# A two-layer hybrid attention block: dividing by the softmax sums after the product with the values

## The chip, the cores and the metric

The kernel runs on one core of one Trainium2 chip. The metric is the device time of one execution in microseconds (us). Three runs of the kernel before gave 601.19, 601.36 and 601.63 us, median 601.36. A core has a matrix engine (PE in the rows; PEld is its loading of the stationary operand), VectorE (DVE), ScalarE (ACT), GpSimd (POOL), SyncE (SP) that issues nearly all DMAs here, and 16 DMA engines. Every engine works through its own queue in order and waits for others by semaphores.

## The reference

Two layers of width 1024 over 256 tokens, in fp32. Each layer norms x, projects it to 2824 columns, runs three mixers side by side, projects their outputs back, and adds an MLP (1024 to 4096 to 1024, squared relu). The mixers are block attention ("moba", 6 heads of 64; with 256 tokens and blocks of 256 it is plain causal attention), a chunked linear recurrence ("mlstm", 4 heads), and sliding-window attention ("swa", 6 query heads on 2 key heads, window 128, with a sink per head). The change is in the two softmax mixers:

```
p = softmax(concat([s_sel, s_own]))          # moba: causal rows of 256 keys
o = einsum('bhql,bhld->bhqd', p, v)
...
p = softmax(concat([s, sink]))[..., :-1]     # swa: the sink is in the sum alone
o = einsum('bnkgqj,bnjkd->bnqkgd', p, vb)
```

Queries and keys are rms-normed per head and rotated before. Since the sum of a row of numerators is one number per query and head, dividing the numerators by it or dividing the product by it gives the same result.

## The kernel before, in words

**Weights.** All weight matrices come from HBM in units of up to 512 KB by one queue (SP). Each unit is split into a high part (ScalarE, a rounded copy, line 258) and a low part (VectorE, a subtraction, line 265), and each product is three matmuls: high by high, high by low, low by high (`three`, lines 613 to 615). The same split is made of the activations. There are eight buffers for high parts and seven for low ones.

**The order.** The program is written as many generators (one for each projection part, head, pair of heads, block of the MLP). A `Scheduler` (lines 127 to 230) with a model of each engine's costs and latencies (`LATENCY`, `ISSUE`, `SWITCH`) picks at each step the operation that can start first by its model, and among those that can start within a short time of it the one with the lowest rank. The result is one fixed instruction order for each engine; on the chip only semaphores hold. Generators of layer 1 have ranks 1000 above those of layer 0. The splits of weight units have rank -20 if the unit is the next one to be used, and 90 otherwise, in either layer (`split_rank`, line 393); the first five units have about -50.

**A pair of heads** (`pair`, line 1093, and `head`, line 1142): twelve pairs in all, three of moba and three of swa in each layer. TensorE makes the scores of both heads, each head in 64 rows of the array. For each head, VectorE scales, masks and takes the row maximum with one custom operation for each of the two query blocks (128 and 256 keys); the scale is a negated inverse root, `nrq`, made by a multiplication by -1 of `rq`. ScalarE takes the exponentials and their sums `su`; in swa the exponential of the sink is added. VectorE takes the reciprocals, and the numerators are multiplied by them in place: two operations for a head, of 128 and 256 columns, on VectorE or on ScalarE, whichever the model has free. TensorE turns the three 128x128 tiles (`to_T`, line 679), ScalarE copies them back to SBUF. The product with the values (`values`, line 1125) then takes 64 columns of the values as the stationary operand and streams the turned numerators past it, 256 and 128 columns, the two heads side by side in the two halves of the array's columns. The result is already turned, [2 heads x 64, 256 queries], and is split at once into the operand of the output projection.

**Around the pairs.** While pairs wait for VectorE and ScalarE, TensorE works on the later projection parts and on the first chunks of the output projection (`mix`, line 1187). When `mix` is done, x is updated (VectorE), turned (`turn`, line 568, TensorE, rank -29) and the MLP starts (`up_first`).

**Roots** (`inverse_root`, line 518): exp(-0.5 ln v) on ScalarE, then one Newton step in three small VectorE operations. `roots` (line 1028) makes those of the queries and keys and then `nrq`.

Of the kernel before, what the change touches and what calls it, by code (L numbers as in the profile page):

```python
# [13 lines left out]
AF = mybir.ActivationFunctionType  # L14
OP = mybir.AluOpType
# [5 lines left out]
HD = 64  # L21
# [102 lines left out]
            self.cur = None  # L124


LATENCY = {"PE": 0.20, "ACT": 0.145, "DVE": 0.13, "POOL": 0.15, "DMA": 1.0}
ISSUE = {"PE": 0.235, "ACT": 0.0, "DVE": 0.0, "POOL": 0.0, "DMA": 0.0}
SWITCH = 0.2
SOON = {"PE": 0.08, "ACT": 0.2, "DVE": 0.05, "POOL": 0.0, "DMA": 0.0}  # L130


class Scheduler:
# [27 lines left out]
    def run(self):  # L161
        while self.threads:
# [38 lines left out]
            if best is None:  # L201
                if not self.threads:
# [4 lines left out]
            t0, eng = best[0], best[1].engine  # L207
            t, th, op = min((c for c in ready if c[2].engine == eng and c[0] <= t0 + SOON[eng]),
                            key=lambda c: c[1].rank())
            self.now = max(self.now, t0)  # L210
            op.fn()
            end = t + op.cost * (1 + (eng == "PE" and t < self.cold))
# [22 lines left out]
def tile_hybrid_block(ctx: ExitStack, tc: tile.TileContext, x, xT, smalls, w_in, w_out, w_up,  # L235
# [36 lines left out]
    def stt(waits, o, a, s, b, op0, op1):  # L272
        return dve(waits, free_size(o),
                   lambda: V.scalar_tensor_tensor(o, a, s, b, op0=op0, op1=op1), pointers=(s,),  # L274
                   bank=bank_of(a, b))
# [6 lines left out]
        return (yield tt([t] + waits, lo, src, f32(hi), OP.subtract).ranked(rank))  # L282

    def dma(waits, nbytes, o, i, eng=None):
        return Op("DMA", nbytes / 360e3, waits, lambda: (eng or nc.sync).dma_start(o, i))

    PS = buffers("ps", 8, [128, 512], F32, pp)
    TMP = buffers("tmp", 6, [128, 512])
# [84 lines left out]
    def load_units():  # L373
        for k, u in enumerate(units):
# [15 lines left out]
            u.t = yield dma([t], u.n * 512, dst, u.src)  # L390
            u.there.signal(u.t)

    def split_rank(k):
        u = units[k]
        if k < 5:
            return -50 + u.kc0
        return lambda: -20 if k < in_use[0] + URGENT else 90

    def split_units():
        for k, u in enumerate(units):  # L400
# [97 lines left out]

    def small_loads(l, after):

        yield Wait(*after)
        g = tab[l][:, T_GB:T_SINK].rearrange("p (s i d) -> p s i d", s=2, i=4)
        t = max(e.t for e in after)
        for k, o in enumerate((cg, sg)):
            for i in range(4):
                t = yield dve([t], 128, lambda k=k, o=o, i=i: V.scalar_tensor_tensor(
                    o[:, i], rope_t[:, k], 1.0 if i % 2 else HD ** -0.5,
                    g[:, k, i, None, :].to_broadcast([128, 2, HD]), op0=OP.mult, op1=OP.mult))
        t = yield ts([t], nsink, tab[l][:, T_SINK:T_BIAS], -1.0, None, OP.mult)
        small_ev[l].signal(t)  # L510
# [7 lines left out]
    def inverse_root(waits, v, k, eps, dst):  # L518


        e, ke = eps or (0.0, 0.0)
        iy, y, t0 = yield from small()
        it, r, t1 = yield from small()
        n = free_size(v)
        y, r = y[:, :n], r[:, :n]
        t = yield act([t0, *waits], y, v, AF.Ln, scale=1.0 / k, bias=e)
        t = yield act([t], y, y, AF.Exp, scale=-0.5)
        t = yield stt([t, t1], r, y, -0.5 / k, y, OP.mult, OP.mult)
        t = yield stt([t], r, v, ke, r, OP.add, OP.mult)
        t = yield stt([t], dst, r, 1.5, y, OP.add, OP.mult)  # L530
        SMALL.put(iy, t)
        SMALL.put(it, t)
        return t
# [168 lines left out]
    for b in range(2):  # L702
        G.memset(vaug[b][:, :, 64:65], 1.0)
    rq = {k: const(f"rq_{k}", [128, 2, 12]) for k in "ms"}
    nrq = {k: const(f"nrq_{k}", [128, 2, 6]) for k in "ms"}
    ssq = {k: const(f"ssq_{k}", [128, 2, 12]) for k in "ms"}
    gcol = const("gcol", [128, 2, 4])
    ecol = const("ecol", [128, 2, 4])
# [3 lines left out]
    class Layer:  # L712
        def __init__(self, l, x_in):
            self.l, self.p, self.x_in = l, plan[l], x_in
            self.h1 = [[Event() for _ in range(KC)] for _ in range(2)]
            self.h2 = [[Event() for _ in range(KC)] for _ in range(2)]
            self.y = [Event(2 if c in (3, 4) else 1) for c in range(8)]
            self.yb = [None] * 4
            self.yuses = [0] * 4
            self.x_mid, self.x_out = ([[Event() for _ in range(4)] for _ in range(2)]  # L720
                                      for _ in range(2))

            groups = (0, 1, 2, "s")
            self.qT = {k: Event(2) for k in ("sq", "sk", 0, 1, 2)}
            self.vv = {k: Event(2) for k in ("mv", "sv", "va", "sig")}
            self.lq = [Event(), Event()]
            self.gates_in = Event(2)
            self.rows, self.cols, self.ecol = Event(), Event(), Event()
            self.row = Event()
            self.ssq = {k: [Event(2 if k == "s" else 1) for _ in range(2)] for k in groups}  # L730
            self.rq = {k: [Event(), Event()] for k in groups}
            self.nrq = {k: [Event(), Event()] for k in groups}
# [295 lines left out]
        def roots(self, g, tb):  # L1028

            yield Wait(self.ssq[g][tb], self.st[tb])  # L1030
            st = stat[1][tb]
            k, a, n, nq = ("s", 0, 8, 6) if g == "s" else ("m", 4 * g, 4, 2)
            r = rq[k][:, tb, a:a + n]
            t = yield from inverse_root([self.ssq[g][tb], self.st[tb]], ssq[k][:, tb, a:a + n],
                                        float(HD), (st[:, 1:2], st[:, 3:4]), r)
            self.rq[g][tb].signal(t)
            t = yield ts([t], nrq[k][:, tb, a // 2:a // 2 + nq], r[:, 0:nq], -1.0, None, OP.mult)
            self.nrq[g][tb].signal(t)

        def moba_part(self, i, tb):  # L1040

# [51 lines left out]
        def pair(self, swa, i, gate, prio):  # L1093

            heads = (i, i + 3) if swa else (2 * i, 2 * i + 1)
            qT, kT = (sqT, skT) if swa else (mT[:, 0], mT[:, 1])
            evs = [self.qT[k] for k in (("sq", "sk") if swa else (i,))]
# [16 lines left out]

            t = yield pe([tp for _, tp in banks] + evs, 0.66, scores, "rows")
            pT = {}
            for h, (ip, _) in zip(heads, banks):
                sch.add(prio + h, self.head(swa, h, pT, done, ip, t))  # L1120
            yield Wait(done, vev)
            iy, ty = yield Get(PS)
            yps = PS.tiles[iy]

            def values():
                for o, blk, cols in ((slice(0, 256), 0, slice(0, 256)),
                                     (slice(128, 256), 1, slice(256, 384))):
                    for n, h in enumerate(heads):
                        d = (n if swa else h) * HD
                        T.matmul(yps[64 * n:64 * n + 64, o], vv[blk][:, d:d + HD],  # L1130
                                 MID.tiles[pT[h]][:, cols], start=blk == 0, stop=blk == 1)

            t = yield pe([done, ty, vev], 0.68, values, "columns").ranked(prio)
            for h in heads:
                MID.put(pT[h], t)
            gate.put(ig, t)
            hi, lo, ty = yield from self.y_tile(c)
            t = yield from split([t, ty], hi, lo, yps[:, 0:256])
            PS.put(iy, t)
            self.y[c].signal(t)  # L1140

        def head(self, swa, h, pT, done, ip, t):
# [5 lines left out]
            nm, su, es = sm[:, 0:2], sm[:, 2:4], sm[:, 4:6]  # L1148
            cuts = (slice(0, 128), slice(128, 384))
            g, hq = ("s", h % 3 * 2 + h // 3) if swa else ("m", h)  # L1150
            done_q = self.nrq["s" if swa else h // 2]
            mask, least = (mask_s, nsink[:, h:h + 1]) if swa else (mask_m, -NEG)
            yield Wait(*done_q)

# [1 line left out]
            for k, cut in enumerate(cuts):  # L1156
                w = [t, t0, tm, *done_q] + ([small_ev[self.l]] if swa else [])
                t = yield dve(w, cut.stop - cut.start + 60, lambda k=k, cut=cut: V.tensor_tensor_reduce(  # L1158
                    p[:, cut], ps[:, cut], mask[:, cut], nrq[g][:, k, hq:hq + 1], least,
                    OP.add, OP.min, nm[:, k:k + 1]), pointers=(nrq[g],), bank=bank_of(ps))  # L1160
            PS.put(ip, t)
            tk = t
            for k, cut in enumerate(cuts):
                t = yield act([tk], p[:, cut], p[:, cut], AF.Exp, bias=nm[:, k:k + 1],
                              scale=-1.0, accum_out=su[:, k:k + 1])
            if swa:
                te = yield act([tk], es, nm, AF.Exp, bias=tab[self.l][:, T_SINK + h:T_SINK + h + 1])
                t = yield tt([te, t], su, su, es, OP.add)
            t = yield dve([t], 16, lambda: V.reciprocal(su, su))
            tn = []  # L1170
            for k, cut in enumerate(cuts):
                a, b = p[:, cut], su[:, k:k + 1]
                tn.append((yield ts([t], a, a, b, None, OP.mult).either(
                    act([t], a, a, AF.Copy, scale=b))))
            t = max(tn)
            SMALL.put(i, t)
# [6 lines left out]
            done.signal(t)  # L1183

# [264 lines left out]
```

## Time and profile before

| | us |
|---|---|
| median of three runs | 601.36 |
| the profiled execution | 601.11 |
| its span, first to last instruction | 599.2 |
| TensorE busy (matmuls) | 592.1 |
| TensorE loading stationary operands | 536.1 |
| VectorE busy | 421.4 |
| ScalarE busy | 350.7 |
| DMA, mean | 172 GB/s |

In the page, busy times of matmuls are modelled and overlap: a matmul that is shown with 0.28 us can have its successor 0.12 us later. What a matmul takes of the engine is therefore read from the distance between the starts of neighbours in the timeline, not from its own duration. An fp32 matmul that isn't split in high and low parts shows as two records.

### The profile page before, as it was taken

How to read it: one execution, taken by the hardware profiler on the slowest of the kernel's cores; microseconds unless marked ns; L12 is line 12 of the kernel's file. 1: busy time of each engine (PE TensorE's matmuls, PEld its weight loads, DVE VectorE, ACT ScalarE, POOL GpSimd, SP SyncE). 2: the span in 40 equal slices, each digit the busy share in tenths (PEclk: the TensorE clock that was granted, in tenths of full speed). 3: DMA queues.
4: the chain of work that ended last, by engine and by line, in shares of the span. 5: the costliest groups of instructions: out<-in, count | busy, mean ns of one | idle time of the engine just before them, and what ended most of it. 6: DMA issues, size and time to landing. Idle time of an engine off the chain costs nothing.

```text
span 599.2 us, 10813 instructions
## 1 busy us (share of the span) xinstructions
PE 592.1 (99%) x4057; PEld 536.1 (89%) x4057; DVE 421.4 (70%) x1027; ACT 350.7 (59%) x780; POOL 3.4 (1%) x12
## 2 busy tenths in 40 slices
PE   8999999999999999999999999999999999999997
PEld 7999987799989989989899999778999999999986
DVE  7999999797627627627489999958856456356452
ACT  6866896786615625626386768757745246246240
POOL 2000000000000000000000000000000000000000
PEclk8999999999999999999999999999999999999999
DMA  9938345356637637637455654113866285385311
GB/s 321 341 97 239 99 145 183 109 185 212 205 111 239 214 111 244 208 120 263 140 150 142 203 191 151 52 65 107 287 205 210 76 274 168 126 272 168 116 68 71
DMA packets 48724, 103.18 MB, mean 172 GB/s; under 512 B 3520, under 2 KB 17088, under 8 KB 48672
## 3 DMA queue, kind: packets, MB, share of 16 engines
q1 hardware_dynamic: 48256, 101.95, 52.1%
q8 instruction: 32, 0.52, 0.4%
q0 software_dynamic: 128, 0.40, 0.2%
q14 instruction: 20, 0.16, 0.1%
q10 hardware_dynamic: 288, 0.15, 0.1%
HBM read 101.43 MB, written 1.05 MB: 171 GB/s over the span
## 4 chain that ended last, share of the span: by engine, by line
PE 93%; DVE 3%; DMA 2%; ACT 1%; issue 0%; SPq 0%; ACTq 0%
PE ps L613 29%; PE ps L615 28%; PE ps L614 28%; PE ps L687 2%; PE ps L1130 2%; PE ps L1114 1%; DMA xs<-in_x_dram 1%; PE ps L582 1%; DMA mid<-in_xT_dram 1%; DVE wlo L265 1%; ACT whi L258 1%; PE ps L924 1%; DVE mid L1158 0%; PE ps L899 0%; PE ps L945 0%
## 5 line engine op out<-in xcount | busy, mean ns | idle before, releaser
L265 DVE TENSOR_TENSOR wlo<-raw,whi 128x512 fp32r<-128x512 f32 (+3 forms) x304 | 234.8, 811 | 78.3 <-PE ps L614 45.7
L258 ACT ACTIVATE whi<-raw 128x512 fp32r<-128x512 f32 (+3 forms) x304 | 204.9, 725 | 72.7 <-PE ps L615 69.0
L613 PE MATMUL ps<-hT,whi 128*128 128x256 f32 x576 | 162.1, 281 | 0.0
L614 PE MATMUL ps<-lT,whi 128*128 128x256 f32 x576 | 161.5, 280 | 0.0
L615 PE MATMUL ps<-hT,wlo 128*128 128x256 f32 x576 | 161.3, 280 | 0.0
L613 PE MATMUL ps<-whi,fh 128*128 128x512 f32 (+1 forms) x352 | 134.0, 381 | 0.0
L615 PE MATMUL ps<-whi,fl 128*128 128x512 f32 (+1 forms) x352 | 131.5, 373 | 0.0
L614 PE MATMUL ps<-wlo,fh 128*128 128x512 f32 (+1 forms) x352 | 131.3, 373 | 0.0
L613 PEld LDWEIGHTS ps<-hT,whi 128*128 128x128 f32 x576 | 108.5, 188 | 0.8
L614 PEld LDWEIGHTS ps<-lT,whi 128*128 128x128 f32 x576 | 108.5, 188 | 0.8
L615 PEld LDWEIGHTS ps<-hT,wlo 128*128 128x128 f32 x576 | 108.6, 188 | 0.0
L613 PE MATMUL ps<-whi,hT 128*128 128x256 f32 (+2 forms) x256 | 79.4, 310 | 0.8 <-DVE fl L274 0.5
L614 PE MATMUL ps<-wlo,hT 128*128 128x256 f32 (+2 forms) x256 | 76.6, 299 | 0.7 <-DVE wlo L265 0.7
L613 PEld LDWEIGHTS ps<-whi,fh 128*128 128x128 f32 x352 | 66.2, 188 | 12.5 <-issue 2.2
L615 PEld LDWEIGHTS ps<-whi,fl 128*128 128x128 f32 x352 | 66.2, 188 | 12.5
L615 PE MATMUL ps<-whi,lT 128*128 128x256 f32 (+2 forms) x256 | 76.5, 299 | 0.0
L614 PEld LDWEIGHTS ps<-wlo,fh 128*128 128x128 f32 x352 | 66.2, 188 | 10.4
L258 ACT ACTIVATE tmp<-ps 128x512 f32<-128x512 f32 (+1 forms) x36 | 19.8, 550 | 69.5 <-PE ps L615 69.5
L265 DVE TENSOR_TENSOR tmp<-tmp 128x512 f32<-128x512 f32 (+1 forms) x32 | 20.9, 655 | 48.8 <-ACT tmp L258 48.8
L613 PEld LDWEIGHTS ps<-whi,hT 128*128 128x128 f32 x256 | 49.0, 191 | 3.3 <-issue 1.5
L614 PEld LDWEIGHTS ps<-wlo,hT 128*128 128x128 f32 x256 | 49.0, 191 | 1.5 <-DVE wlo L265 1.2
L615 PEld LDWEIGHTS ps<-whi,lT 128*128 128x128 f32 x256 | 48.9, 191 | 0.4 <-DVE lT L274 0.4
(146 smaller groups left out, 507.2 us busy)
## 6 DMA issues: line engine op xcount, KB each, us to landing
raw<-in_w_up_dram SPq DMA_DIRECT2D x64, 512.0 KB, 4.6
raw<-in_w_down_dram SPq DMA_DIRECT2D x64, 512.0 KB, 4.8
raw<-in_w_in_dram SPq DMA_DIRECT2D x24, 512.0 KB, 4.7
raw<-in_w_out_dram SPq DMA_DIRECT2D x16, 512.0 KB, 3.6
raw<-in_w_in_dram SPq DMA_DIRECT2D x16, 384.0 KB, 4.0
raw<-in_w_in_dram SPq DMA_DIRECT2D x7, 520.0 KB, 5.8
xs<-in_x_dram SPq DMA_DIRECT2D x2, 512.0 KB, 7.1
mid<-in_xT_dram SPq DMA_DIRECT2D x7, 128.0 KB, 5.7
```

What stands on the lines that cost most here:

```text
L258: lambda: A.activation(o, i, func, **kw), bank)
L265: return dve(waits, free_size(o), lambda: V.tensor_tensor(o, a, b, op=op), bank=bank_of(a, b))
L582: T.transpose(ps[:, k * 128:k * 128 + 128], xs[:, tb, c:c + 128], ident)
L613: T.matmul(ps, s[0], m[0], start=start, stop=False)
L614: T.matmul(ps, s[0], m[1], start=False, stop=False)
L615: T.matmul(ps, s[1], m[0], start=False, stop=stop)
L687: T.transpose(ps[:, cs], src[:, cs], ident)
L924: T.matmul(PS.tiles[ip][:, o], lqk[b, 2 + c, ks], lqk[b, c, qs], start=o.start == 0, stop=o.start > 0)
L1114: T.matmul(PS.tiles[ip][:, o], qT[b, i, q], kT[b, kc, k], start=o.start == 0, stop=o.start > 0)
L1130: T.matmul(yps[64 * n:64 * n + 64, o], vv[blk][:, d:d + HD], MID.tiles[pT[h]][:, cols], start=blk == 0, stop=blk == 1)
```

## The change

It does four things.

1. **The division.** The numerators are no longer multiplied by the reciprocals. They are turned as they are; the product with the values now takes 128x128 tiles of the turned numerators as the stationary operand and streams 64 columns of values past it, three matmuls for a head (one for the first query block, two for the second), in the whole array. The result is [128 queries, (block, head) x 64]. One VectorE operation multiplies it by the reciprocals of both heads and both blocks, broadcast over 64 columns; two further turns (`to_T(t, y, 2)`) bring it into the layout of the output projection. Sums and reciprocals are made once for a pair.
2. **The roots.** The Newton step gives the negated root, the key tables are made with the opposite sign, and `nrq` with its multiplications goes. The first step of the Newton iteration becomes a Square on ScalarE.
3. **The planner's model.** Latency of a DMA 2.2 instead of 1.0 us, its rate 330 instead of 360 KB per us. A long ScalarE or VectorE operation of rank above -25 gives way to one of rank -25 or less that will be ready within 0.5 us.
4. **Ranks of splits.** Units of layer 1 that aren't the next to be used get rank 1090 instead of 90.

```diff
-LATENCY = {..., "DMA": 1.0}
+LATENCY = {..., "DMA": 2.2}
+URGENTLY = -25
...
+            if eng in ("ACT", "DVE") and op.cost > 0.3 and th.rank() > URGENTLY:
+                soon = [c for c in ready if c[2].engine == eng and c[1].rank() <= URGENTLY
+                        and t < c[0] < min(t + 0.5, t + op.cost - 0.2)]
+                if soon:
+                    t, th, op = min(soon, key=lambda c: c[0])
...
-        return Op("DMA", nbytes / 360e3, waits, ...)
+        return Op("DMA", nbytes / 330e3, waits, ...)
...
-        return lambda: -20 if k < in_use[0] + URGENT else 90
+        rest = 90 + 1000 * (k >= of_first)
+        return lambda: -20 if k < in_use[0] + URGENT else rest
...
-        t = yield stt([t, t1], r, y, -0.5 / k, y, OP.mult, OP.mult)
-        t = yield stt([t], r, v, ke, r, OP.add, OP.mult)
-        t = yield stt([t], dst, r, 1.5, y, OP.add, OP.mult)
+        t = yield act([t, t1], r, y, AF.Square, scale=(0.5 / k) ** 0.5)
+        if eps:
+            t = yield stt([t], r, v, ke, r, OP.add, OP.mult)
+            t = yield stt([t], dst, r, 1.5, y, OP.subtract, OP.mult)
...
-            t = yield ts([t], nrq[k][:, tb, a // 2:a // 2 + nq], r[:, 0:nq], -1.0, None, OP.mult)
...
             def values():
-                for o, blk, cols in ((slice(0, 256), 0, slice(0, 256)),
-                                     (slice(128, 256), 1, slice(256, 384))):
+                for qb in range(2):
                     for n, h in enumerate(heads):
                         d = (n if swa else h) * HD
-                        T.matmul(yps[64 * n:64 * n + 64, o], vv[blk][:, d:d + HD],
-                                 MID.tiles[pT[h]][:, cols], start=blk == 0, stop=blk == 1)
-            t = yield pe([done, ty, vev], 0.68, values, "columns").ranked(prio)
+                        for kb in range(qb + 1):
+                            c = (qb + kb) * 128
+                            T.matmul(yps[:, qb * 128 + n * HD:qb * 128 + n * HD + HD],
+                                     MID.tiles[pT[h]][:, c:c + 128], vv[kb][:, d:d + HD],
+                                     start=kb == 0, stop=kb == qb)
+            t = yield pe([done, ty, vev], 0.68, values).ranked(prio)
...
+            tr = yield dve(w, 16, lambda: V.reciprocal(sums[:, 0:4], sums[:, 0:4]))
+            im, tm = yield Get(MID)
+            y = MID.tiles[im][:, 0:256]
+            t = yield tt([t, tr, tm], y.rearrange("p (g d) -> p g d", d=HD),
+                         yps[:, 0:256].rearrange("p (g d) -> p g d", d=HD),
+                         sums[:, 0:4, None].to_broadcast([128, 4, HD]), OP.mult)
+            iy, ps, t = yield from to_T(t, y, 2)
             hi, lo, ty = yield from self.y_tile(c)
-            t = yield from split([t, ty], hi, lo, yps[:, 0:256])
+            t = yield from split([t, ty], hi, lo, ps[:, 0:256])
...
-            t = yield dve([t], 16, lambda: V.reciprocal(su, su))
-            tn = []
-            for k, cut in enumerate(cuts):
-                a, b = p[:, cut], su[:, k:k + 1]
-                tn.append((yield ts([t], a, a, b, None, OP.mult).either(
-                    act([t], a, a, AF.Copy, scale=b))))
```

## Rows read from the trace of the kernel before

**Rows 1.** The page: span; busy time, share and instructions of each engine; the granted clock of TensorE in 40 slices; the shares of the chain that ended last.

```profile
span 599.2 us, 10813 instructions
...
PE 592.1 (99%) x4057; PEld 536.1 (89%) x4057; DVE 421.4 (70%) x1027; ACT 350.7 (59%) x780; POOL 3.4 (1%) x12
...
PEclk8999999999999999999999999999999999999999
...
PE 93%; DVE 3%; DMA 2%; ACT 1%; issue 0%; SPq 0%; ACTq 0%
```

**Rows 2.** Who TensorE waited for, whole span: us in total, times, longest.

```profile
PE ps L462 <- DVE wz L456: 1.2, 1, 1.2
PE ps L582 <- DVE xs L265: 0.8, 1, 0.8
PE ps L614 <- DVE wlo L265: 0.7, 1, 0.7
PE ps L613 <- DVE fl L274: 0.5, 1, 0.5
PE ps L613 <- ACT hT L258: 0.3, 1, 0.3
```

**Rows 3.** Busy time in stretches (us from the start): the pairs of layer 0, its MLP with the start of layer 1, the pairs of layer 1. Columns: length, then busy us and count of PE, PEld, DVE, ACT, POOL, granted clock, DMA share, GB/s.

```profile
60.00:118.00 58.00, 58.00 (x406) 47.99 (x406) 54.16 (x214) 45.47 (x138) 0.00 (x0) 1.00 0.42 134
118.00:310.00 192.00, 192.00 (x1253) 174.67 (x1252) 117.88 (x205) 102.59 (x190) 0.00 (x0) 1.00 0.56 184
...
354.00:416.00 62.00, 60.69 (x416) 49.67 (x416) 52.32 (x207) 45.39 (x142) 0.00 (x0) 1.00 0.32 103
```

**Rows 4.** TensorE's timeline around one product with the values (L1130): start, duration, operation.

```profile
75.57 0.28 PE L614 MATMUL ps<-wlo,hT 128*128 128x256 f32 x1
75.69 0.28 PE L615 MATMUL ps<-whi,lT 128*128 128x256 f32 x1
75.90 0.87 PE L1130 MATMUL ps<-mid,sv 128*64 128x256 f32 x8
76.70 0.39 PE L613 MATMUL ps<-whi,hT 128*128 128x256 f32 x1
76.92 0.29 PE L614 MATMUL ps<-wlo,hT 128*128 128x256 f32 x1
77.05 0.28 PE L615 MATMUL ps<-whi,lT 128*128 128x256 f32 x1
```

**Rows 5.** The same for the values of the mlstm heads (L943 to L945), three matmuls for each head: 128x128 stationary out of a `mid` buffer, 65 columns streamed, fp32.

```profile
57.50 0.33 PE L943 MATMUL ps<-vaug,mid 128*128 128x65 f32 x2
57.66 0.39 PE L944 MATMUL ps<-vaug,mid 128*128 128x65 f32 x2
...
58.11 0.39 PE L943 MATMUL ps<-vaug,mid 128*128 128x65 f32 x2
58.33 0.39 PE L944 MATMUL ps<-vaug,mid 128*128 128x65 f32 x2
...
58.78 0.39 PE L943 MATMUL ps<-vaug,mid 128*128 128x65 f32 x2
```

**Rows 6.** The same around three turns (L687) amid projections.

```profile
72.18 0.28 PE L615 MATMUL ps<-whi,lT 128*128 128x256 f32 x1
72.30 0.49 PE L687 MATMUL ps<-ident,mid 128*128 128x128 f32 x3
72.55 0.36 PE L613 MATMUL ps<-whi,hT 128*128 128x256 f32 x1
72.75 0.28 PE L614 MATMUL ps<-wlo,hT 128*128 128x256 f32 x1
```

**Rows 7.** Groups of TensorE by line and shape: count | busy us, mean ns | idle before.

```profile
L1130 PE MATMUL ps<-mid,mv 128*64 128x256 f32 x24 | 3.9, 404 | 0.0
...
L945 PE MATMUL ps<-vaug,mid 128*128 128x65 f32 x16 | 3.1, 275 | 0.0
```

**Rows 8.** Groups of VectorE and ScalarE by line and shape, same columns: the multiplications of the numerators on VectorE (first two rows), a multiplication of 256 columns read from PSUM, a negation of roots, a small ScalarE operation.

```profile
L269 DVE TENSOR_SCALAR mid<-mid,small 128x256 f32<-128x256 f32 x21 | 7.3, 346 | 0.0
...
L269 DVE TENSOR_SCALAR mid<-mid,small 128x128 f32<-128x128 f32 x22 | 6.2, 282 | 0.2
...
L265 DVE TENSOR_TENSOR mid<-ps,sig 128x256 f32<-128x256 f32 x4 | 1.6, 411 | 0.0
...
L269 DVE TENSOR_SCALAR nrq_m<-rq_m 128x2 f32<-128x2 f32 x12 | 1.9, 158 | 0.0
...
L258 ACT ACTIVATE small<-small 128x4 f32<-128x4 f32 x20 | 4.1, 204 | 1.5 <-DVE small L269 1.1
```

**Rows 9.** The timeline in layer 1 where TensorE waits for `fl`; in brackets the engine's idle time before, and what ended it.

```profile
370.74 1.22 DVE L265 TENSOR_TENSOR wlo<-raw,whi 128x1024 fp32r<-128x1024 f32 x1
...
371.88 0.34 DVE L274 SCALAR_TENSOR_TENSOR fl<-ps,tab,fh 128x128 fp32r<-128x128 f32 x1
...
372.27 0.39 PE L613 MATMUL ps<-whi,hT 128*128 128x256 f32 x1 [0.51 <-DVE fl L274]
```

**Rows 10.** Busy time in three stretches of the start, columns as in rows 3.

```profile
8.00:9.00 1.00, 1.00 (x6) 1.00 (x6) 0.89 (x3) 0.47 (x2) 0.00 (x0) 0.50 1.08 384
...
10.00:11.00 1.00, 1.00 (x6) 1.00 (x6) 1.00 (x2) 1.00 (x3) 0.00 (x0) 0.50 1.12 354
...
12.00:14.00 2.00, 2.00 (x16) 2.00 (x17) 2.00 (x5) 1.96 (x5) 0.00 (x0) 1.00 1.02 401
```

More of the change, by code (lines that the diff above doesn't have):

```diff
@@ L124, in step @@
             self.cur = None
-LATENCY = {"PE": 0.20, "ACT": 0.145, "DVE": 0.13, "POOL": 0.15, "DMA": 1.0}
+LATENCY = {"PE": 0.20, "ACT": 0.145, "DVE": 0.13, "POOL": 0.15, "DMA": 2.2}
 ISSUE = {"PE": 0.235, "ACT": 0.0, "DVE": 0.0, "POOL": 0.0, "DMA": 0.0}
 SWITCH = 0.2
+URGENTLY = -25
 SOON = {"PE": 0.08, "ACT": 0.2, "DVE": 0.05, "POOL": 0.0, "DMA": 0.0}
@@ L284, in dma @@
     def dma(waits, nbytes, o, i, eng=None):
-        return Op("DMA", nbytes / 360e3, waits, lambda: (eng or nc.sync).dma_start(o, i))
+        return Op("DMA", nbytes / 330e3, waits, lambda: (eng or nc.sync).dma_start(o, i))
     PS = buffers("ps", 8, [128, 512], F32, pp)
@@ L391, in load_units @@
             u.there.signal(u.t)
+    of_first = len(units) // 2
     def split_rank(k):
@@ L506, in small_loads @@
                 t = yield dve([t], 128, lambda k=k, o=o, i=i: V.scalar_tensor_tensor(
-                    o[:, i], rope_t[:, k], 1.0 if i % 2 else HD ** -0.5,
+                    o[:, i], rope_t[:, k], -1.0 if i % 2 else HD ** -0.5,
                     g[:, k, i, None, :].to_broadcast([128, 2, HD]), op0=OP.mult, op1=OP.mult))
@@ L527, in inverse_root @@
         t = yield act([t], y, y, AF.Exp, scale=-0.5)
-        t = yield stt([t, t1], r, y, -0.5 / k, y, OP.mult, OP.mult)
-        t = yield stt([t], r, v, ke, r, OP.add, OP.mult)
-        t = yield stt([t], dst, r, 1.5, y, OP.add, OP.mult)
+        t = yield act([t, t1], r, y, AF.Square, scale=(0.5 / k) ** 0.5)
+        if eps:
+            t = yield stt([t], r, v, ke, r, OP.add, OP.mult)
+            t = yield stt([t], dst, r, 1.5, y, OP.subtract, OP.mult)
+        else:
+            t = yield stt([t], r, v, -1.0, r, OP.mult, OP.mult)
+            t = yield stt([t], dst, r, 1.5, y, OP.add, OP.mult)
         SMALL.put(iy, t)
@@ L704, in tile_hybrid_block @@
     rq = {k: const(f"rq_{k}", [128, 2, 12]) for k in "ms"}
-    nrq = {k: const(f"nrq_{k}", [128, 2, 6]) for k in "ms"}
     ssq = {k: const(f"ssq_{k}", [128, 2, 12]) for k in "ms"}
@@ L731, in __init__ @@
             self.rq = {k: [Event(), Event()] for k in groups}
-            self.nrq = {k: [Event(), Event()] for k in groups}
             self.st = [Event() for _ in range(2)]
@@ L1031, in roots @@
             st = stat[1][tb]
-            k, a, n, nq = ("s", 0, 8, 6) if g == "s" else ("m", 4 * g, 4, 2)
+            k, a, n = ("s", 0, 8) if g == "s" else ("m", 4 * g, 4)
             r = rq[k][:, tb, a:a + n]
@@ L1036, in roots @@
             self.rq[g][tb].signal(t)
-            t = yield ts([t], nrq[k][:, tb, a // 2:a // 2 + nq], r[:, 0:nq], -1.0, None, OP.mult)
-            self.nrq[g][tb].signal(t)
         def moba_part(self, i, tb):
@@ L1118, in pair @@
             pT = {}
-            for h, (ip, _) in zip(heads, banks):
-                sch.add(prio + h, self.head(swa, h, pT, done, ip, t))
+            i4, sums, t4 = yield from small()
+            for n, (h, (ip, _)) in enumerate(zip(heads, banks)):
+                sch.add(prio + h, self.head(swa, h, n, pT, sums, done, ip, max(t, t4)))
             yield Wait(done, vev)
@@ L1136, in pair, with head @@
             gate.put(ig, t)
+            w = [t]
+            if swa:
+                w = [t, (yield tt([done], sums[:, 0:4], sums[:, 0:4], sums[:, 4:8], OP.add))]
+            tr = yield dve(w, 16, lambda: V.reciprocal(sums[:, 0:4], sums[:, 0:4]))
[4 more added lines that the diff above has]
+                         sums[:, 0:4, None].to_broadcast([128, 4, HD]), OP.mult)
+            PS.put(iy, t)
+            SMALL.put(i4, t)
+            iy, ps, t = yield from to_T(t, y, 2)
+            MID.put(im, t)
             hi, lo, ty = yield from self.y_tile(c)
-            t = yield from split([t, ty], hi, lo, yps[:, 0:256])
+            t = yield from split([t, ty], hi, lo, ps[:, 0:256])
             PS.put(iy, t)
             self.y[c].signal(t)
-        def head(self, swa, h, pT, done, ip, t):
+        def head(self, swa, h, n, pT, sums, done, ip, t):
             ps = PS.tiles[ip]
@@ L1147, in head @@
             i, sm, t0 = yield from small()
-            nm, su, es = sm[:, 0:2], sm[:, 2:4], sm[:, 4:6]
+            nm = sm[:, 0:2]
             cuts = (slice(0, 128), slice(128, 384))
-            g, hq = ("s", h % 3 * 2 + h // 3) if swa else ("m", h)
-            done_q = self.nrq["s" if swa else h // 2]
+            g, hq = ("s", h % 3 * 2 + h // 3) if swa else ("m", h // 2 * 4 + h % 2)
+            done_q = self.rq["s" if swa else h // 2]
             mask, least = (mask_s, nsink[:, h:h + 1]) if swa else (mask_m, -NEG)
@@ L1158, in head @@
                 t = yield dve(w, cut.stop - cut.start + 60, lambda k=k, cut=cut: V.tensor_tensor_reduce(
-                    p[:, cut], ps[:, cut], mask[:, cut], nrq[g][:, k, hq:hq + 1], least,
-                    OP.add, OP.min, nm[:, k:k + 1]), pointers=(nrq[g],), bank=bank_of(ps))
+                    p[:, cut], ps[:, cut], mask[:, cut], rq[g][:, k, hq:hq + 1], least,
+                    OP.add, OP.min, nm[:, k:k + 1]), pointers=(rq[g],), bank=bank_of(ps))
             PS.put(ip, t)
@@ L1164, in head @@
                 t = yield act([tk], p[:, cut], p[:, cut], AF.Exp, bias=nm[:, k:k + 1],
-                              scale=-1.0, accum_out=su[:, k:k + 1])
+                              scale=-1.0, accum_out=sums[:, 2 * k + n:2 * k + n + 1])
+            te = t
             if swa:
-                te = yield act([tk], es, nm, AF.Exp, bias=tab[self.l][:, T_SINK + h:T_SINK + h + 1])
-                t = yield tt([te, t], su, su, es, OP.add)
-            t = yield dve([t], 16, lambda: V.reciprocal(su, su))
-            tn = []
-            for k, cut in enumerate(cuts):
-                a, b = p[:, cut], su[:, k:k + 1]
-                tn.append((yield ts([t], a, a, b, None, OP.mult).either(
-                    act([t], a, a, AF.Copy, scale=b))))
-            t = max(tn)
-            SMALL.put(i, t)
+                es = sums[:, 4:8].rearrange("p (b n) -> p b n", n=2)
+                te = yield act([tk], es[:, :, n], nm, AF.Exp,
+                               bias=tab[self.l][:, T_SINK + h:T_SINK + h + 1])
+            SMALL.put(i, te)
             it, pt, t = yield from to_T(t, p, 3)
@@ L1182, in head @@
             pT[h] = im
-            done.signal(t)
+            done.signal(max(t, te))
         def mix(self, tb, n):
```

## The prediction

> **What bounds the kernel.** I read the page's busy times and chain first. TensorE is busy 592.1 of 599.2 us, VectorE 70%, ScalarE 59%, and the chain that ended last runs through TensorE for 93% of the span [rows 1]. A busy TensorE may still hide waits, because the busy time of a matmul is modelled, so the second view is the list of who TensorE waited for: five waits, 3.5 us in all, of which 2.2 us lie in the start-up (1.2, 0.7 and 0.3) and 1.3 us in layer 1 (0.5 for `fl`, 0.8 for the last update of x) [rows 2]. The third view is the distance between the starts of neighbouring matmuls, and in the projections around the changed code they follow each other every 0.12 us, without holes [rows 4, 6]. So the kernel is a queue of matmuls that never runs dry after the first microseconds. What counts is the TensorE time that the change adds or removes; VectorE and ScalarE count only where TensorE waits for them. The stages differ in that: VectorE is busy 54 of 58 us in the pairs of layer 0 and 52 of 62 in those of layer 1, and 118 of 192 us in the MLP between them, and TensorE is full in the first and the last of these three to within 1.3 us [rows 3].
>
> **The division, TensorE.** One product before takes eight records: 75.90 to 76.70, 0.80 us. The matmul ahead of it keeps the engine 0.21 us (75.69 to 75.90) where its like keeps it 0.12, and the one behind it 0.22 (76.70 to 76.92): 0.09 and 0.10 us for going into the half-array mode and out of it. Together 0.99 us [rows 4]. There are twelve of these: the moba row counts 24 records of 256 columns, which is 2 heads x 2 records x 3 pairs x 2 layers, and swa has as many pairs [rows 7].
>
> After, a pair has three fp32 matmuls for each of two heads, six in all, twelve records, each with a 128x128 stationary tile from a `mid` buffer and 64 columns streamed. The trace has this shape but for one column: the mlstm values, 128x128 from `mid`, 65 columns. One head's three matmuls (six records) take 58.11 to 58.78, 0.67 us, so 0.112 us a record [rows 5]; and sixteen records stand for the eight heads of L945, so two records a matmul here too [rows 7]. A pair takes 12 x 0.112 = 1.34 us. They are in whole-array mode, and I add nothing for going in and out.
>
> The two new turns: three turns delay the projection from 72.30 to 72.75, 0.45 us, less the 0.12 that the one delayed matmul would have taken, 0.33, so 0.11 each [rows 6]; 0.22 us a pair.
>
> The sum for a pair is 1.34 + 0.22 - 0.99 = +0.57 us, for twelve pairs **+6.8 us**. Nothing hides it: it is on the engine that never waits. Its bounds: from below, the first two records of a block take 0.16 us (57.50 to 57.66) instead of 0.22 [rows 5], since the first load ran behind an earlier matmul; one such record a pair makes 1.28 and a sum of +6.1. From above, 0.08 us for going out (a 256-column matmul behind turns takes 0.20 instead of 0.12 [rows 6]), +7.8. I take +6.8.
>
> The Trainium skill has a rule on this exchange: "TensorEngine Tiling (Array Packing)", section "When to Use Tiling", says that with a streamed dimension of 64 or less one should swap stationary and streamed operand and tile the columns twice. The kernel before does that, and the change undoes it; the page's section "Theoretical Speedup" gives up to 2x for it, by which, as an estimate, the product would go from 0.99 to 1.98 us and the sum to +14.5. By that rule the time would be 614.7; the trace bears out the direction and a smaller factor: 1.34 against 0.99 [rows 4, 5].
>
> **The division, VectorE and ScalarE.** 43 multiplications go from VectorE, 7.3 + 6.2 = 13.5 us, and the other five of 48 from ScalarE; twelve of 256 columns out of PSUM come, 12 x 0.411 = 4.9 us [rows 8]. The negations of the moba roots take 1.9 us away [rows 8]. One step of each of 24 inverse roots (12 moba, 4 swa, 4 of the norms, 4 mlstm) moves to ScalarE: 24 x 0.204 = 4.9 us there [rows 8]. VectorE loses some 10 us of 421 and more with the small ones. TensorE waited for it 2.0 us in all (0.8, 0.7, 0.5; the first 1.2 is the clearing before the warm-up) [rows 2], so this relief is worth at most those waits. It also shortens each head's way from the exponentials to its turns, but TensorE fills that time with other matmuls already. Behind the product the way to the output projection grows by the new operation (0.41) and two turns. The wait it adds stands on TensorE's own queue: the turns wait for VectorE, and behind them are the matmuls of projections and `mix`.
>
> **Ranks of splits, long operations giving way.** The wait of 0.5 us for `fl` is of this kind: a split of 1024 columns of a later unit started on VectorE at 370.74, took 1.22 us, and the 0.34 us operation that TensorE needed came behind it [rows 9]. With rank 1090 such a split stands behind the pairs of layer 1, as rank 90 does in layer 0. I take **-0.5**. What it costs if the cover goes: a split that comes too late stops TensorE for as long as it takes, 1.2 us; layer 0 has worked under the same relative ranks and its 58 us of pairs show no wait [rows 2, 3]. The 0.8 us wait for the last update of x I leave, since nothing says which matmuls the planner will find to lay there; gone, it is -0.8.
>
> **Latency of DMAs in the model.** No instruction changes, only the order in the first 25 us can. At 8 to 11 us the granted clock is 0.50 (the 1.2 GHz level), and 1.00 at 12 us; before the fall TensorE had stood still between its warm-up and the first split units [rows 2, 10]. Another order can mend this or lengthen it. Bounds: 1.7 us (half of some 3.4 us) and the two waits, 1.0, at best; the same 2.7 us at worst, if the clock falls for twice as long and the waits double. I take 0, and +-1.0 for the likeliest case.
>
> **Sum.** 601.1 (the profiled execution) + 6.8 - 0.5 = 607.4. That execution lies 0.25 us below the median of 601.36; I keep the sum in its own terms, and take 0.4 off for half of the 0.8 us wait: **607.0 us**, 5.6 above the median. Less than 0.2% either way (1.2 us) I count as the same.
>
> **Rivals.**
> 1. *The loads hide.* If the engine pulls the load of every stationary tile behind the matmul before it, a record takes only its streaming, about 0.06 us as the first of a block shows (0.16 less 0.11) [rows 5]. A pair is then 0.7 + 0.22 - 0.99 = -0.07, the sum -0.8, and with the waits gone (-1.3) the time is about 599: faster. It decides from about 0.065 us a record. Against it: all later records of the same shape took 0.112, in every block. 4%. The skill's page on tiling, section "Instruction Overhead", speaks for it, since it charges a matmul of few columns by a floor near 60 columns and nothing for its stationary tile; the trace doesn't agree, with 0.112 us where streaming alone would give half.
> 2. *All waits go.* The planner's better model takes the two waits in layer 1 (1.3), and start-up waits and low clock (2.7): 601.1 + 6.8 - 4.0 = 603.9, still slower. 10%.
> 3. *New waits.* VectorE runs behind the plan, and the new turns stand in TensorE's queue: with 0.5 us (the wait of rows 9) at every second pair, +3.0 and no -0.5: 610.9. For it speaks that the planner still prices the product at 0.68 us, so its picture slips; against it, that a slower TensorE gives VectorE time, and that the turns of the numerators stand in the same way behind ScalarE and VectorE and none of them is in the list of waits [rows 2]. 10%.
> 4. *The division costs little in wall time because TensorE isn't the bound in the pairs.* Then VectorE's relief of some 5 us a layer would show and the time come out near 600. Against it: no waits in 58 us where VectorE was 93% busy [rows 2, 3]. 2%.
>
> The forecast has 74%, with its own range of 605.2 to 608.8. The range 603.8 to 609.8 takes in most of rivals 2 and 3 and the bounds of the terms. Faster 0.05 (rivals 1 and 4), same 0.03, slower 0.92.
>
> **What would show it.** The products with the values: twelve records of 128x128 by 64 columns, 1.34 us from first to last and next; two turns more for a pair, 144 turns instead of 120; VectorE's busy time near 405 us; no wait for `fl` in layer 1; PE waits still under 5 us. A record of 0.06 us would make the sum wrong at its root, and so would many new waits of TensorE for the multiplication before the turns.

## The result, and the profile after

The changed kernel takes 607.7 us in the median (607.07 to 607.89, four runs), beside 601.5 us for the kernel before: a ratio of 1.0101, 95% interval 1.0084 to 1.0119. It is slower by 6.2 us. The profiled execution took 607.7 us too, with a span of 605.9, so 6.6 us more than the profiled execution before.

The page of the changed kernel, the lines of [rows 1]:

```profile
span 605.9 us, 10893 instructions
...
PE 597.3 (99%) x4129; PEld 548.7 (91%) x4129; DVE 412.7 (68%) x939; ACT 353.4 (58%) x798; POOL 3.4 (1%) x12
...
PE 98%; DVE 1%; issue 0%; POOL 0%; POOLq 0%
```

TensorE has 72 records more: 12 x 12 instead of 12 x 8 for the products, and 24 turns. VectorE has 88 instructions less and is busy 8.7 us less, and the chain that ended last is TensorE for 98%, after 93% before. Whether VectorE's work was on the path at all is tested below (`e3_before_no_mult`).

TensorE's timeline around one product of the changed kernel, to be held against [rows 4]:

```profile
85.58 0.28 PE L630 MATMUL ps<-whi,lT 128*128 128x256 f32 x1
85.70 1.45 PE L1144 MATMUL ps<-sv,mid 128*128 128x64 f32 x12
86.96 0.36 PE L628 MATMUL ps<-whi,hT 128*128 128x256 f32 x1
87.16 0.28 PE L629 MATMUL ps<-wlo,hT 128*128 128x256 f32 x1
```

Twelve records last from 85.70 to 86.96, 1.26 us. The matmul ahead of them is not held up (0.12 us), the one behind is shown 0.20 us long by its successor's start, 0.08 more than its like. Together 1.34 us, where [rows 4] gave 0.99. Where turns follow a product and not a projection (77.73 to 79.01 us, for one), there are 1.28 us and nothing for the way out.

Who TensorE waited for in the changed kernel, as in [rows 2] (L472 is the warm-up, L629 and L628 the first split units, L597 the turns of x):

```profile
PE ps L597 <- DVE xs L272: 1.6, 2, 0.8
PE ps L472 <- DVE wz L466: 1.2, 1, 1.2
PE ps L629 <- DVE wlo L272: 1.1, 1, 1.1
PE ps L628 <- ACT whi L265: 1.1, 1, 1.1
```

The wait for `fl` is gone. The wait for the last update of x, which layer 1 alone had before, is there in both layers. In layer 0 it stands here:

```profile
123.85 0.40 PE L630 MATMUL ps<-whi,fl 128*128 128x512 f32 x1
...
125.03 0.66 PE L597 MATMUL ps<-ident,xs 128*128 128x128 f32 x4 [0.78 <-DVE xs L272]
```

From the start of the last matmul of the output projection to the first turn are 1.18 us, where the next matmul would have come after 0.23: 0.95 us lost, of which the list shows the 0.78 behind the modelled end of the matmul.

In the start, TensorE's granted clock is at its lower level (0.50, the 1.2 GHz level) as it was before, in the columns of [rows 10]:

```profile
8.00:9.00 1.00, 1.00 (x7) 1.00 (x7) 0.99 (x4) 0.40 (x1) 0.00 (x0) 0.50 1.06 380
```

### The profile page after: what moved, and what is told of

It reads as the page before. It is cut to its first block, busy times and chain, and to the rows that moved or that the text cites. A ratio compares the mean times of both kernels' runs of the same rounds, so it can differ in the third digit from the quotient of the medians.

```text
span 605.9 us, 10893 instructions
## 1 busy us (share of the span) xinstructions
PE 597.3 (99%) x4129; PEld 548.7 (91%) x4129; DVE 412.7 (68%) x939; ACT 353.4 (58%) x798; POOL 3.4 (1%) x12
## 4 chain that ended last, share of the span: by engine, by line
PE 98%; DVE 1%; issue 0%; POOL 0%; POOLq 0%
PE ps L628 30%; PE ps L629 29%; PE ps L630 29%; PE ps L702 3%; PE ps L1144 3%; PE ps L1126 2%; PE ps L597 1%; PE ps L937 0%; PE ps L912 0%; PE ps L957 0%; PE ps L958 0%; PE ps L956 0%; DVE ident L478 0%; DVE xs L272 0%; PE ps L761 0%
## 5 line engine op out<-in xcount | busy, mean ns | idle before, releaser
L628 PE MATMUL ps<-hT,whi 128*128 128x256 f32 x576 | 162.1, 281 | 0.0
L629 PE MATMUL ps<-lT,whi 128*128 128x256 f32 x576 | 161.4, 280 | 0.0
L628 PE MATMUL ps<-whi,fh 128*128 128x512 f32 (+1 forms) x352 | 134.1, 381 | 0.0
L629 PE MATMUL ps<-wlo,fh 128*128 128x512 f32 (+1 forms) x352 | 131.4, 373 | 0.0
L628 PEld LDWEIGHTS ps<-hT,whi 128*128 128x128 f32 x576 | 108.4, 188 | 0.8
L629 PEld LDWEIGHTS ps<-lT,whi 128*128 128x128 f32 x576 | 108.4, 188 | 0.7
L628 PE MATMUL ps<-whi,hT 128*128 128x256 f32 (+2 forms) x256 | 80.6, 315 | 1.1 <-ACT whi L265 1.1
L629 PE MATMUL ps<-wlo,hT 128*128 128x256 f32 (+2 forms) x256 | 76.4, 299 | 1.1 <-DVE wlo L272 1.1
L628 PEld LDWEIGHTS ps<-whi,fh 128*128 128x128 f32 x352 | 66.2, 188 | 11.1 <-issue 0.7
L629 PEld LDWEIGHTS ps<-wlo,fh 128*128 128x128 f32 x352 | 66.3, 188 | 10.5
L628 PEld LDWEIGHTS ps<-whi,hT 128*128 128x128 f32 x256 | 48.9, 191 | 3.3 <-ACT whi L265 1.4
L629 PEld LDWEIGHTS ps<-wlo,hT 128*128 128x128 f32 x256 | 49.0, 192 | 1.5 <-DVE wlo L272 1.3
```

The source lines that it names most:

```text
L628: T.matmul(ps, s[0], m[0], start=start, stop=False)
L629: T.matmul(ps, s[0], m[1], start=False, stop=False)
```

## The experiments

Theory: TensorE is full, so the change costs the TensorE time of the new product and the new turns, and everything else counts only through TensorE's few waits. Rivals: the planner's model, ranks and roots make the kernel slower and the division is free; TensorE has slack among the pairs, so that VectorE's time counts; a record of the new product costs its streaming and not the load of its tile.

### The two halves of the change

`e1_division_alone` puts the new `pair` and `head` into the kernel before; `e2_rest_alone` puts the old ones into the changed kernel. The edits are those of the change, save that the scores are scaled by whichever buffer has the negated root. In e1, against the changed kernel:

```diff
-            g, hq = ("s", h % 3 * 2 + h // 3) if swa else ("m", h // 2 * 4 + h % 2)
-            done_q = self.rq["s" if swa else h // 2]
+            g, hq = ("s", h % 3 * 2 + h // 3) if swa else ("m", h)
+            done_q = self.nrq["s" if swa else h // 2]
```

In e2, against the kernel before:

```diff
-            g, hq = ("s", h % 3 * 2 + h // 3) if swa else ("m", h)
-            done_q = self.nrq["s" if swa else h // 2]
+            g, hq = ("s", h % 3 * 2 + h // 3) if swa else ("m", h // 2 * 4 + h % 2)
+            done_q = self.rq["s" if swa else h // 2]
```

> The kernel before with the division behind the product alone; roots, planner's model and ranks as before. TensorE theory: 12 pairs x (1.28 + 0.22 + about 0.05 for going out - 0.99) = +6.7 us over the kernel before, so 608.2, within 1 us. Rival, that the planner and the roots make the kernel slower and the division costs nothing: 601 to 602.

> The changed kernel with the old division: numerators multiplied before they are turned, old product; negated roots, planner's model and ranks as changed. TensorE theory: as the kernel before less the wait for fl (0.5) and within 1 us for the start: 600.0 to 602.0. Rival, planner and roots cost: 606 to 608.

Measured: e1 608.48 us beside 601.07 of the kernel before, ratio 1.0123 (1.0107 to 1.0138). The division alone makes the kernel slower by all of the loss and more; the rival that blames planner and roots falls. e2 took 598.47 us, ratio 0.9955 (0.9943 to 0.9968): the rest of the change makes the kernel before faster, by 2.6 us instead of about 0.5, and so lies below the expected range of 600.0 to 602.0. It beats both kernels. TensorE's waits in e2:

```profile
PE ps L472 <- DVE wz L466: 1.2, 1, 1.2
PE ps L629 <- DVE wlo L272: 1.1, 1, 1.1
PE ps L628 <- ACT whi L265: 0.4, 1, 0.4
```

All are of the start-up: neither `fl` nor the update of x stops TensorE any more.

The two halves don't add up to the whole: +7.4 and -2.6 make +4.8, and the changed kernel has +6.2. With the division in place the rest of the change takes off only 0.8 us (608.48 to 607.70). TensorE's waits in e1 show why:

```profile
PE ps L582 <- DVE xs L265: 1.6, 2, 0.8
PE ps L462 <- DVE wz L456: 1.2, 1, 1.2
PE ps L614 <- DVE wlo L265: 1.0, 2, 0.8
PE ps L613 <- ACT hT L258: 0.4, 1, 0.4
PE ps L776 <- DVE small L269: 0.2, 1, 0.2
```

The first line is the update of x in both layers, and it stays in the changed kernel; the others are of the first 25 us. The wait for `fl` is already gone in e1, without the new ranks, so in the changed kernel the ranks had no wait behind the start left to take away but these two, and took neither.

### Which part of the rest it is

`e8_before_ranks` gives the kernel before the new ranks of the splits and nothing else; `e10_before_dma` gives it the new latency and rate of a DMA in the planner and nothing else.

The edit of e8:

```diff
-        return lambda: -20 if k < in_use[0] + URGENT else 90
+        rest = 90 + 1000 * (k >= len(units) // 2)
+        return lambda: -20 if k < in_use[0] + URGENT else rest
```

The edit of e10:

```diff
-LATENCY = {..., "DMA": 1.0}
+LATENCY = {..., "DMA": 2.2}
...
-        return Op("DMA", nbytes / 360e3, ...)
+        return Op("DMA", nbytes / 330e3, ...)
```

> The kernel before with the lower rank of layer 1's splits alone. If the split of 1.22 us in front of the fl operation made the 0.5 us wait in layer 1, the wait goes and the time is 600.7 to 601.2. Rival: another order, another wait of that size, 601.5; or splits that come too late, over 602.5.

> The kernel before with the planner's new latency and rate of a DMA alone. If the order of the start decides something, it shows in the first 25 us: by my reading of the forecast at most 1 us either way, 600.2 to 602.2. Rival, that the new model orders the whole kernel better: under 600, with the waits of layer 1 gone.

Measured: e8 598.96 us beside 601.18, ratio 0.9962 (0.995 to 0.9975), below the expected range. The ranks bring the kernel before 2.2 us, and so nearly all that e2 gains; what roots, the rule for long operations and the DMA model add to it (598.47 against 598.96, in two sessions) is too little to tell, and the first two were not run alone. e10 601.94 beside 601.28, ratio 1.0011 (1.0003 to 1.002): the DMA model alone costs 0.7 us, within the range. But it changed more than the first 25 us. Among the pairs of layer 0, where the kernel before has no wait, e10 has one of 1.1 us:

```profile
89.97 0.88 PE L687 MATMUL ps<-ident,mid 128*128 128x128 f32 x6 [1.11 <-DVE fl L265]
```

e8's gain is more than the one wait that I had traced to a split. Its list of waits has neither of the two of layer 1:

```profile
PE ps L463 <- DVE wz L457: 1.2, 1, 1.2
PE ps L615 <- DVE wlo L265: 0.7, 1, 0.7
PE ps L614 <- ACT hT L258: 0.4, 1, 0.4
```

The pairs of layer 1 in the view of [rows 3], for e8:

```profile
354.00:416.00 62.00, 62.00 (x436) 52.15 (x435) 56.13 (x205) 49.18 (x147) 0.00 (x0) 1.00 0.39 130
```

There, 436 records of TensorE fall in the 62 us instead of 416, without a hole. The wait for `fl` had a split in front of it [rows 9]. The wait for the update of x had none: in the kernel before the turns simply follow the last matmul of the output projection,

```profile
414.14 0.40 PE L615 MATMUL ps<-whi,fl 128*128 128x512 f32 x1
...
415.32 0.66 PE L582 MATMUL ps<-ident,xs 128*128 128x128 f32 x4 [0.78 <-DVE xs L265]
```

and in e8 matmuls of the MLP stand between the two:

```profile
413.03 0.39 PE L616 MATMUL ps<-whi,fl 128*128 128x512 f32 x1
...
413.26 0.28 PE L614 MATMUL ps<-hT,whi 128*128 128x256 f32 x1
...
414.67 0.60 PE L583 MATMUL ps<-ident,xs 128*128 128x128 f32 x4
```

That the order came out so with the new ranks is what the run shows; which split had kept those matmuls back was not traced.

### VectorE's share

`e3_before_no_mult` leaves out the multiplications of the numerators (so the numerators go into the product unnormed), and keeps their price in the plan:

```diff
-                tn.append((yield ts([t], a, a, b, None, OP.mult).either(
-                    act([t], a, a, AF.Copy, scale=b))))
+                o1 = ts([t], a, a, b, None, OP.mult)
+                o2 = act([t], a, a, AF.Copy, scale=b)
+                o1.fn = o2.fn = lambda: None
+                tn.append((yield o1.either(o2)))
```

> The kernel before with its 48 multiplications of the numerators by the reciprocals left out (the plan still counts them, so the order is the same; the output isn't normed). TensorE theory: nothing but a wait or two, 600.5 to 601.7, though VectorE is rid of some 13 us. Rival, that VectorE is the bound among the pairs: some 5 us a layer, 591 to 596.

Measured: 600.91 beside 601.07 us, ratio 0.9997 (0.9988 to 1.0006). The page of e3:

```profile
PE 592.6 (99%) x4057; PEld 537.0 (89%) x4057; DVE 414.1 (69%) x984; ACT 349.3 (58%) x775; POOL 3.3 (1%) x12
```

43 instructions of VectorE and five of ScalarE are gone, and the time stays. So the work that the division was moved to save is worth nothing in this kernel, and the rival of a VectorE-bound stage falls.

### The price of a product, old and new

`e5_before_twice` and `e6_after_twice` issue every product twice in a row, at an unchanged price in the plan. The result is the same, since the second one starts its sums anew.

```diff
             def values():
+              for _ in range(2):
...
```

> The kernel before with each product with the values issued twice in a row (same result, same plan). In layer 1 of the kernel before two products stand in a row, and the second takes 0.65 us. TensorE theory: 12 x 0.65 = +7.8 us, 609.3, within 1. Rival, that TensorE has slack among the pairs: under +3.

> The changed kernel with each product issued twice in a row (same result, same plan). TensorE theory, with the loads of 128x128 fp32 tiles setting the pace: 12 x 12 x 0.112 = +16.1 us over the changed kernel, 623.8, within 1. Rival, that a record costs its streaming of about 0.055 and the rest was overlap at the edges: +8, 615.7. Rival slack: under +5.

Measured: e5 608.84 beside 601.18 us, +7.7, or 0.64 us for a product without its change of mode (0.65 expected). e6 623.6 us, 15.9 more than the changed kernel's 607.7, or 1.33 us for a product: 0.110 us for each of 144 records (0.112 expected). TensorE takes every record in full, so it has no slack among the pairs, and the rival with half the price is out. In e6's timeline 24 records, from their start to the turns behind them, take 2.62 us:

```profile
78.28 2.79 PE L1145 MATMUL ps<-sv,mid 128*128 128x64 f32 x24
80.90 0.39 PE L702 MATMUL ps<-ident,mid 128*128 128x128 f32 x2
```

`e7_after_wide` streams 128 columns instead of 64 past each tile: the values of both heads. The half that belongs to the other head isn't read.

```diff
-                            T.matmul(yps[:, qb * 128 + n * HD:qb * 128 + n * HD + HD],
-                                     MID.tiles[pT[h]][:, c:c + 128], vv[kb][:, d:d + HD],
+                            d = (0 if swa else heads[0]) * HD
+                            o = qb * 256 + n * 128
+                            T.matmul(yps[:, o:o + 128],
+                                     MID.tiles[pT[h]][:, c:c + 128], vv[kb][:, d:d + 2 * HD],
...
+            own = yps.rearrange("p (b k d) -> p b k d", b=2, d=HD)[:, :, 0:4:3]
```

> The changed kernel with 128 columns streamed in place of 64 (both heads' values; the half that belongs to the other head is not read). Theory that the load of the stationary tile sets the pace: a turn streams 128 columns and takes 0.109, so a record stays at 0.11 and the time at 607.7, within 0.8. Rival, that the columns set the pace: a record doubles to 0.22, +15 us, 623.

Measured: 607.87 us, 0.2 from the changed kernel, with twice the columns. So the columns don't set the pace. The groups of e7 by line and shape show the wider records, as many as before:

```profile
L1146 PE MATMUL ps<-sv,mid 128*128 128x128 f32 x72 | 9.0, 275 | 0.0
L1146 PE MATMUL ps<-mv,mid 128*128 128x128 f32 x72 | 9.0, 275 | 0.0
```

What sets it is the load of the stationary tile. TensorE's loads around the product of the changed kernel shown above:

```profile
85.59 1.43 PEld L1144 LDWEIGHTS ps<-sv,mid 128*128 128x128 f32 x12
86.93 0.19 PEld L628 LDWEIGHTS ps<-whi,hT 128*128 128x128 f32 x1
```

Twelve loads start within 1.34 us, one every 0.112, and the matmuls follow at that pace. Only the first record of a block, whose load starts ahead of the block, keeps the engine for its columns alone: in the traces the second one starts 0.055 us after it with 64 columns, and 0.108 with 128 (e7). A fixed price of any record is not the reason, since that first one is cheaper, and in e5 eight records with tiles of 64 columns took 0.64 us, 0.08 each. No run changed the width of the tile alone.

The Trainium skill gives a price for such a load in "TensorE: Matmul & The Clock Gate", section "LDWEIGHTS (loading the stationary operand)": it takes the number of its columns divided by 1.2, in ns, which for 128 columns gives an estimate of 107 ns. The runs agree, with 110 to 112 ns a record.

### The turns, and the planner's price

`e4_after_no_turns` leaves out the two turns (the unturned product goes into the output projection):

```diff
-            iy, ps, t = yield from to_T(t, y, 2)
-            MID.put(im, t)
             hi, lo, ty = yield from self.y_tile(c)
-            t = yield from split([t, ty], hi, lo, ps[:, 0:256])
-            PS.put(iy, t)
+            t = yield from split([t, ty], hi, lo, y)
+            MID.put(im, t)
```

> The changed kernel without the two turns of the normed product (its operand of the output projection is then the unturned one; the output is another). TensorE theory: 24 turns x 0.11 = 2.6 us less than the changed kernel, 605.1, within 0.8. Rival, that TensorE waits for the multiplication ahead of the turns: 4 us less or more, under 604.

Measured: 603.98 us, 3.7 less than the changed kernel: more than the turns alone and outside the range of the theory, and by its number just on the rival's side (under 604). The trace settles it. Its waits for the update of x:

```profile
PE ps L597 <- DVE xs L272: 0.8, 1, 0.8
```

One of the two is gone, in layer 1. 2.6 for 24 turns and 0.95 for that wait make 3.6; added up as in the accounts below, e4's pairs are 2.5 us shorter than the changed kernel's, and its waits 0.95. No wait of TensorE for the multiplication ahead of the turns is in the list of the changed kernel above, so the turns cost their own time, and the order that comes out without them has one wait less.

`e9_after_priced` corrects the planner's price of the product:

```diff
-            t = yield pe([done, ty, vev], 0.68, values).ranked(prio)
+            t = yield pe([done, ty, vev], 1.3, values).ranked(prio)
```

> The changed kernel with the planner's price of the product raised from 0.68 to 1.3 us (its measured length); no instruction more or less, another order at most. If the two waits of 0.8 us for the update of x come from the planner's too short price, one or both go and the time is 606.0 to 607.0. If they come from the place of the last product in the order, they stay: 607.5 to 608.

Measured: 606.64 us beside 601.28, ratio 1.0091 (1.0076 to 1.0107), 1.1 less than the changed kernel. The waits again show one for the update of x, in layer 0, and none in layer 1:

```profile
124.68 0.65 PE L597 MATMUL ps<-ident,xs 128*128 128x128 f32 x4 [0.78 <-DVE xs L272]
```

So a price that is half of the truth did cost a wait in layer 1. Why that of layer 0 stays, no run here tells; it stays open.

### The accounts

This adds up, for the profiled executions, the distance from each TensorE record to the next by what the record is (worked out from the traces; a projection or MLP matmul counts with its usual distance, what goes beyond it as an edge, or as a wait where it is over 0.3 us):

```
us                                     before  after   e1     e2     e8
start, to the first mlstm scores         48.3   48.5   48.8   49.1   48.6
projections and MLP, usual distance     491.4  491.4  491.4  491.4  491.4
pairs: scores, products, turns, edges    43.9   50.1   50.8   42.6   43.0
waits behind the start                    1.6    1.9    1.9    0.0    0.0
others                                    9.1    9.1    9.1    9.1    9.1
```

The rest of each span, 4.9 us, is 1.2 before TensorE's first record and 3.7 from its last one to the end. The changed kernel loses 6.2 us in the pairs, 0.3 in waits and 0.2 in the start: 6.7 together. e1 loses 6.9, 0.3 and 0.5. e2 and e8 gain the two waits of the kernel before, 1.6, and 0.9 to 1.3 in the pairs, at the edges, and are 0.3 (e8) and 0.8 (e2) longer in the start. The edges shrink in part because the scores of the twelve pairs stand in nine blocks there instead of eleven, and pairs in one block share the change of mode (the changed kernel has nine too, e1 eleven).

Differences in the start are not the edits' alone. e3, whose plan is that of the kernel before, took 49.4 us there: its granted clock was still at the lower level where [rows 10] has 1.00:

```profile
12.00:14.00 2.00, 2.00 (x11) 2.00 (x10) 2.00 (x5) 1.89 (x5) 0.00 (x0) 0.50 1.04 403
```

## Why the prediction was right

The forecast was 607.0 us and slower; it came out at 607.7, slower by 6.2 against a forecast of 5.6 (above 601.36; with a fourth run the median before is 601.5). The bound, the sign and the price of a record are shown by the runs. That the total came so near is in part luck, since the errors of the terms have different signs: on the spans, the pairs came out 0.6 below their term, the waits 1.2 above theirs and the start 0.2 above.

- *TensorE is the bound, and the sum is made on it.* Shown by e5 and e6, where added records cost their full time, and by e3, where removed VectorE work costs nothing.
- *The product and the turns, +6.8.* The accounts give +6.2 for the changed kernel and +6.9 for the division alone. By its terms: a record 0.110 (e6) where I took 0.112, and the first one of each block half of that, which I had set as the lower bound; the way out of the block, 0.08, which I had set as the upper bound, is there where a projection follows and not where turns do.
- *The shape.* Reading the price from the mlstm product with 65 columns, and not from the column count, was the step that decided the sign. e6 and e7 bear it out: 0.110 us a record, with 64 columns and with 128.
- *Ranks of splits, -0.5.* In the kernel before, the wait for `fl` goes with the ranks, and the size was off: -2.2 by themselves (e8), because both waits of layer 1 went and the edges shrank. I had traced one wait and left the other. In the changed kernel the term stands for something else: there the division alone already ends the wait for `fl` (e1), and all the rest together takes 0.8 us from e1, in the pairs and the start.
- *The wait for the update of x, -0.4 as half of 0.8.* Wrong in sign: the changed kernel has it in both layers. The accounts of waits say -0.9 in the forecast (0.5 and 0.4) and +0.3 in the trace.
- *The DMA model, 0 within 1.* e10 was 0.7 us slower, within the bounds, and the low clock at the start that I had put into them is still there in the changed kernel. That the order can change in the first 25 us only was wrong: e10 has a new wait at 90 us.
- *VectorE near 405 us.* It was 412.7. The durations of VectorE operations overlap in the rows: in [rows 9] one starts at 371.88 that stands behind one that lasts to 371.96, and those of all 1027 add up to 489.7 us where the page has 421.4 busy. So the 43 multiplications with 13.5 us in the groups took only 7.3 us of busy time with them (421.4 to 414.1 in e3).
- *Rivals.* A product at twice its price, 614.7: the factor was about 1.3 (1.28 to 1.34 against 0.99). Without the changes of mode, which fall on the old product alone, it was 2.1 (1.33 in e6 against 0.64 in e5). Hidden loads: out by e6 and e7. All waits go: those of layer 1 did in e2 and e8, while those of the start-up stayed; with the division the wait for the update of x stayed too, and in both layers. New waits: one of 0.95 us, at the end of the output projection and not before the new turns, as the rival had it. VectorE as the bound: out by e3.

## What to carry to other kernels

Before moving work off an engine to save its time, ask which engine waits for it: here 7 us of VectorE's time were worth nothing, while the 0.5 to 0.6 us that each pair added to a full TensorE came through twelve times over. In this kernel an fp32 matmul with a 128x128 stationary tile and 64 or 128 columns cost 0.11 us a record, the pace of its loads; with the 64-wide side stationary in half-array tiles and the long side streamed the same product took 0.99 us instead of 1.28 to 1.34. So price both ways round from rows before choosing. When a change has several parts, time each alone, and then look whether they add up: one rank, which looked like housekeeping, was worth 2.2 us in the kernel before, the division cost three times as much, and beside the division the rest of the change was worth only 0.8.

## What the runs showed of the hardware that I had not expected

Doubling the streamed columns of a 128x128 fp32 matmul from 64 to 128 changed the time of the kernel by 0.2 us in 607.7 (e7), so in such a product half of the columns come free. And the sum of the durations of VectorE instructions says too much: 13.5 us by the groups were 7.3 us of the engine's busy time.
